# A hybrid encoder block in split fp32: each gate and up strip gets its weights at a place of its own

## The chip, the cores and the metric

The kernel runs on one core of one Trainium2 chip. The metric is the device time of one execution in microseconds. A profiled execution gives, beside its own time, a trace of every instruction; the span is the time from the first to the last instruction in it.

## The reference

One encoder block over 256 rows of width 2048: an input projection into four mixers (linear attention, Fourier mixing, long convolution, short convolution), an output projection, a cross attention over 256 memory rows, and a gated feed-forward layer of width 5632, each with a residual sum, and a final norm. All is fp32. What the change touches is the feed-forward layer:

```python
D_MODEL, SEQ, D_FF = 2048, 256, 5632

def rms_norm(x, g):
    xf = x.astype(jnp.float32)
    y = xf * lax.rsqrt(jnp.mean(xf * xf, axis=-1, keepdims=True) + EPS)
    return (y * g.astype(jnp.float32)).astype(x.dtype)

def swiglu(h, w_gate_up, w_down):
    gate, up = jnp.split(h @ w_gate_up, 2, axis=-1)
    return (jax.nn.silu(gate) * up) @ w_down

# in reference(), for the one layer:
x = x + mix @ w_out[l]
x = x + cross_attention(rms_norm(x, norm_g[l, 1]), mem_n, w_xq[l], w_xkv[l], w_xo[l])
x = x + swiglu(rms_norm(x, norm_g[l, 2]), w_gate_up[l], w_down[l])
return rms_norm(x, final_norm_g)
```

## The kernel before, in words

**Split products.** To multiply fp32 numbers with the faster `float32r` matmul, each operand is split into a high part (the value rounded to `float32r`) and a low part (the rest), and three products are added: high by high, high by low, low by high. Activations lie in slots `act` of 512 columns: the high part in columns 0 to 255, the low part in 256 to 511.

**The weight stream.** All weight matrices are cut into blocks of 128 x 128, and laid out in memory in the order in which the kernel takes them (`NBLK` blocks in all, 16 to a slab). `Stream._half` works half a slab at a time, 8 blocks or 1024 columns. For every second half it starts the load of a slab into one of three `raw` buffers from SP's queue (line 83). Then it takes a buffer `wh` and a buffer `wl`, each one of three, and fills them: the high part with a cast on ScalarE (line 104), the low part with a subtraction on VectorE (line 105). A buffer has 1088 columns of 4 bytes, of which 1024 are used; `at` is the column at which the used part starts. It is 0 in the stages listed in `ROWS`, among them everything from the gate and up projection on, and 8 in the others. `Stream.take` hands out the next blocks, and keeps the halves up to two ahead of the one in use (three while a fourth buffer, `extra`, exists, which is before the feed-forward layer).

**Two ways to multiply.** In `gemm` the weights are stationary and the activations stream past them (lines 301 and 302: 512 and 256 columns; lines 298, 299 and 302 in the narrow form: three times 256). In `gemm_rows`, the activations are stationary and a strip of 512 weight columns, four blocks, streams past them. For each of the 16 pieces of depth 128 and each half of the 256 rows, `part_rows` issues three matmuls of 512 columns (lines 346, 347 and 348):

```python
self.nc.tensor.matmul(p[:, :], hi, wh, start=start, stop=False)
self.nc.tensor.matmul(p[:, :], hi, wl, start=False, stop=False)
self.nc.tensor.matmul(p[:, :], lo, wh, start=False, stop=stop)
```

**The feed-forward layer.** `gate_up` goes through 11 pairs of strips: gate columns j x 512 and up columns j x 512. The first pair is taken in one call of `gemm_rows`, gate and up by turns at every depth; all later strips have a call of their own, gate before up:

```python
for j in range(1, DFF // 512):
    gate(self.gemm_rows("w_gate_up", [j * 512], self.h3)[0])
    up(j, self.gemm_rows("w_gate_up", [DFF + j * 512], self.h3)[0])
```

A strip is 16 x 4 = 64 blocks, or 8 halves. `gate` applies the activation function on ScalarE (line 757), `up` multiplies on VectorE, transposes (line 764) and writes the result to memory with four transfers from POOL's queue (line 767); `fetch` reads it back and splits it for the down projection (lines 779, 204 and 196). `down` then multiplies with four strips of 512 columns over 44 pieces of depth, again with `part_rows`. The last 32 blocks of the stream lie in buffers of their own (`held`).

The same lines 346 to 348 also serve two short stages earlier on: the values of the cross attention (99 to 202 us) and those of the linear attention (302 to 328 us).

The order of work on each engine is that of the program; `Background` puts side work (norms, transposes, the read-back) between the matmuls by estimated times. Lines 857 and 1119 are two such pieces of side work: small transposes and a small product of the long convolution.

Of the kernel before, what the change touches and what calls it, by code (L numbers as in the profile page):

```python
# [27 lines left out]
FT = DFF // P  # L28
EPS = 1e-6
NBLK = 16 * (40 + 16 + 16 + 32 + 16 + 88) + 16 * FT  # L30
# [6 lines left out]
HELD = 32  # L37

ROWS = ((256, 512), (768, 832), (NBLK - 48 * FT, NBLK))

LATE = 12

# [20 lines left out]
class Stream:  # L63
# [13 lines left out]
    def _half(self):  # L77

        nc, n = self.nc, 8 * len(self.halves)
        if n % 16 == 0:  # L80
            self.raw = self.rawp.tile([P, 2048], F32, name="raw", tag="raw")
            for a, b in zip(CUTS[n], CUTS[n][1:]) if n in CUTS else [(0, 1024), (1024, 2048)] if self.after else [(0, 2048)]:
                (nc.scalar if (n, a) == (0, 0) else nc.sync).dma_start(self.raw[:, a:b], self.W[n // 16][:, a:b])
                if self.after:
                    self.after.pop(0)()
        o = (n % 16) * P
        r = self.raw[:, o:o + 1024]
        if n >= NBLK - HELD:
            parts = []
            for a in (0, 512):  # L90
                wh, wl = self.places.pop(0)
                nc.scalar.copy(wh, r[:, a:a + 512])
                nc.vector.tensor_tensor(out=wl, in0=r[:, a:a + 512], in1=wh.bitcast(F32), op=ALU.subtract)
                parts.append((wh, wl))
            self.bg.dve(1024)
            self.halves.append(parts)
            return
        pool = self.extra if self.extra and len(self.halves) % 4 == 3 else self.wp
        wh, wl = (pool.tile([P, 1088], F32R, name=t, tag=t) for t in ("wh", "wl"))
        at = 0 if any(a <= n < b for a, b in ROWS) else 8  # L100
        wh, wl = wh[:, at:at + 1024], wl[:, at:at + 1024]
        edges = [0, 256, 512, 1024] if n == 0 else [0, 512, 1024] if n == 8 else [0, 1024]
        for a, b in zip(edges, edges[1:]):
            nc.scalar.copy(wh[:, a:b], r[:, a:b])  # L104
            nc.vector.tensor_tensor(out=wl[:, a:b], in0=r[:, a:b], in1=wh[:, a:b].bitcast(F32), op=ALU.subtract)  # L105
        self.bg.dve(1024)
        self.halves.append((wh, wl))
# [1326 lines left out]
```

## Time and profile before

| What | Value |
|---|---|
| Median of 2 runs | 1498.29 us (1498.02 to 1498.56) |
| Profiled execution, its own time | 1498.32 us |
| Its span | 1496.5 us |
| Granted TensorE clock, mean | 0.998 of full |
| TensorE busy | 1485.9 us (99%) |
| Weight loads | 1254.2 us (84%) |
| VectorE busy | 938.3 us (63%) |
| ScalarE busy | 759.3 us (51%) |
| GpSimd busy | 149.7 us (10%) |
| Moved by DMA | 306.11 MB, mean 205 GB/s |

A busy time counts every moment at which an instruction of the engine is under way. The matmuls of TensorE overlap one another, so their durations add up to more than the span that they fill; the distance between the starts of two matmuls tells the pace. The gate and up projection fills 761 to 1248 us, the down projection the rest up to 1488 us.

### The profile page before, as it was taken

What the parts mean: (1) busy time and instruction counts of PE and PEld (TensorE: products, weight loads), DVE (VectorE), ACT (ScalarE), POOL (GpSimd) and SP (SyncE); (2) the same over time, 40 slices, a digit from 0 to 9 for tenths busy, and PEclk for the clock granted to TensorE, in tenths of its full rate; (3) what the DMA queues carried; (4) which work ended last, traced back from release to release, by engine and by line L of the source; (5) the groups of instructions that cost most, each with busy time, mean ns of one, the idle gap of its engine ahead of it and who ended that gap; (6) DMA issues with size and microseconds to landing.
All of it is one profiled execution on the core that took longest, in us unless ns stands there. A gap on an engine that the chain in (4) does not pass through costs nothing.

```text
span 1496.5 us, 19811 instructions
## 1 busy us (share of the span) xinstructions
PE 1485.9 (99%) x7582; PEld 1254.2 (84%) x7582; DVE 938.3 (63%) x1373; ACT 759.3 (51%) x1125; POOL 149.7 (10%) x260
## 2 busy tenths in 40 slices
PE   9999999999999999999999999999999999999997
PEld 8887788889899888888888888888888888888886
DVE  6676778778777767877765554555554456444444
ACT  6565555557545655756544444444444445434344
POOL 0100100000000001200042401111110112000000
PEclk9999999999999999999999999999999999999999
DMA  9975554454546555554567756666666666555554
GB/s 355 347 250 193 189 192 160 167 192 142 183 142 222 188 185 201 193 179 152 189 194 253 239 207 213 216 223 225 209 204 211 220 222 226 185 186 194 197 196 141
DMA packets 56174, 306.11 MB, mean 205 GB/s; under 512 B 9197, under 2 KB 10510, under 8 KB 24464
## 3 DMA queue, kind: packets, MB, share of 16 engines
q1 hardware_dynamic: 45632, 281.11, 54.2%
q0 software_dynamic: 10016, 23.08, 4.9%
q8 instruction: 59, 0.97, 0.3%
q10 hardware_dynamic: 432, 0.66, 0.1%
q14 instruction: 35, 0.29, 0.1%
HBM read 291.18 MB, written 13.63 MB: 204 GB/s over the span
## 4 chain that ended last, share of the span: by engine, by line
PE 97%; ACT 1%; DVE 1%; DMA 0%; issue 0%; SPq 0%; ACTq 0%
PE pg L301 21%; PE pg L346 18%; PE pg L347 17%; PE pg L348 17%; PE pg L302 11%; PE pm L346 1%; PE pm L348 1%; PE pm L347 1%; PE pg L298 1%; PE pg L299 1%; PE pm L301 1%; PE pm L725 1%; PE pm L698 0%; PE pm L302 0%; DMA raw<-in_W 0%
## 5 line engine op out<-in xcount | busy, mean ns | idle before, releaser
L105 DVE TENSOR_TENSOR wl<-raw,wh 128x1024 fp32r<-128x1024 f32 (+1 forms) x503 | 611.6, 1217 | 481.5 <-ACT wh L104 477.1
L104 ACT CAST wh<-raw 128x1024 fp32r<-128x1024 f32 (+1 forms) x503 | 524.3, 1043 | 595.2 <-PE pg L348 396.3
L301 PE MATMUL pg<-act,wh 128*128 128x512 f32 x1296 | 457.7, 395 | 0.3 <-ACT wh L104 0.3
L302 PE MATMUL pg<-act,wl 128*128 128x256 f32 x1472 | 412.4, 280 | 0.2 <-DVE wl L105 0.2
L346 PE MATMUL pg<-wh,act 128*128 128x512 f32 x1008 | 397.1, 394 | 0.0
L347 PE MATMUL pg<-wl,act 128*128 128x512 f32 x1008 | 395.9, 393 | 0.0
L348 PE MATMUL pg<-wh,act 128*128 128x512 f32 x1008 | 392.9, 390 | 0.0
L301 PEld LDWEIGHTS pg<-act,wh 128*128 128x128 f32 x1296 | 243.6, 188 | 54.3 <-ACT wh L104 0.6
L302 PEld LDWEIGHTS pg<-act,wl 128*128 128x128 f32 x1472 | 276.8, 188 | 2.3 <-issue 1.2
L346 PEld LDWEIGHTS pg<-wh,act 128*128 128x128 f32 x1008 | 189.3, 188 | 45.8 <-issue 1.7
L348 PEld LDWEIGHTS pg<-wh,act 128*128 128x128 f32 x1008 | 189.3, 188 | 42.5
L347 PEld LDWEIGHTS pg<-wl,act 128*128 128x128 f32 x1008 | 189.5, 188 | 38.6
L767 POOL DMA_DIRECT2D hidden<-u x88 | 56.9, 654 | 312.1 <-DVE u L764 310.6
L298 PE MATMUL pg<-act,wh 128*128 128x256 f32 x176 | 50.6, 288 | 0.0
L299 PE MATMUL pg<-act,wh 128*128 128x256 f32 x176 | 49.3, 280 | 0.0
L346 PE MATMUL pg<-wh,f 128*128 128x512 f32 x120 | 47.3, 394 | 0.0
L348 PE MATMUL pg<-wh,f 128*128 128x512 f32 x120 | 47.0, 392 | 0.0
L347 PE MATMUL pg<-wl,f 128*128 128x512 f32 x120 | 46.6, 388 | 0.0
L811 POOL DMA_DIRECT2D xrows<-tmp x48 | 27.7, 584 | 130.1 <-DVE tmp L808 126.0
L196 DVE TENSOR_TENSOR tmp<-pg,tmp 128x256 f32<-128x256 f32 x86 | 35.9, 418 | 6.7 <-ACT tmp L308 4.5
L308 ACT COPY tmp<-pg 128x256 f32<-128x256 f32 x85 | 30.9, 365 | 10.9 <-PE pg L302 10.8
L298 PEld LDWEIGHTS pg<-act,wh 128*128 128x128 f32 x176 | 33.2, 188 | 0.2
(272 smaller groups left out, 1239.6 us busy)
## 6 DMA issues: line engine op xcount, KB each, us to landing
raw<-in_W SPq DMA_DIRECT2D x246, 1024.0 KB, 4.9
raw<-in_W SPq DMA_DIRECT2D x11, 512.0 KB, 7.5
hidden<-u POOLq DMA_DIRECT2D x88, 64.0 KB, 3.0
tmp<-hidden POOLq DMA_DIRECT2D x44, 128.0 KB, 4.0
res<-in_xT SPq DMA_DIRECT2D x8, 512.0 KB, 6.0
k<-in_mem SPq DMA_DIRECT2D x8, 256.0 KB, 7.8
k<-in_x SPq DMA_DIRECT2D x8, 256.0 KB, 8.4
keys<-tmp POOLq DMA_DIRECT2D x16, 128.0 KB, 5.8
```

The costliest lines, as they stand in the source:

```text
L104: nc.scalar.copy(wh[:, a:b], r[:, a:b])
L105: nc.vector.tensor_tensor(out=wl[:, a:b], in0=r[:, a:b], in1=wh[:, a:b].bitcast(F32), op=ALU.subtract)
L196: self.nc.vector.tensor_tensor(out=out, in0=a, in1=b, op=op)
L298: self.nc.tensor.matmul(p[:, 0:R], wh, slot[:, 0:R], start=start, stop=False)
L299: self.nc.tensor.matmul(p[:, 0:R], wh, slot[:, R:512], start=False, stop=False)
L301: self.nc.tensor.matmul(p[:, :], wh, slot[:, :], start=start, stop=False)
L302: self.nc.tensor.matmul(p[:, 0:R], wl, slot[:, 0:R], start=False, stop=stop)
L308: self.nc.scalar.copy(t, p[:, R:512])
L346: self.nc.tensor.matmul(p[:, :], hi, wh, start=start, stop=False)
L347: self.nc.tensor.matmul(p[:, :], hi, wl, start=False, stop=False)
L348: self.nc.tensor.matmul(p[:, :], lo, wh, start=False, stop=stop)
L767: nc.gpsimd.dma_start(to[:, :, 32 * a:32 * a + 32], u[32 * a:32 * a + 32, :].rearrange("f (b t) -> f b t", t=32))
```

## The change

A table of 22 places, one for each strip of 512 gate or up columns in the order in which the stream takes them, replaces the single `at` of these strips. The unit is a column of 4 bytes. Everything else, the buffers and their sizes included, stays.

```diff
 ROWS = ((256, 512), (768, 832), (NBLK - 48 * FT, NBLK))
+
+PLACES = (0, 0, 24, 32, 40, 48, 56, 8, 16, 4, 12, 20, 28, 36, 44, 52, 60, 2, 6, 22, 26, 24)
...
         pool = self.extra if self.extra and len(self.halves) % 4 == 3 else self.wp
         wh, wl = (pool.tile([P, 1088], F32R, name=t, tag=t) for t in ("wh", "wl"))
         at = 0 if any(a <= n < b for a, b in ROWS) else 8
+        if 0 <= n - (NBLK - 48 * FT) < 32 * FT:
+            at = PLACES[(n - (NBLK - 48 * FT)) // 64]
         wh, wl = wh[:, at:at + 1024], wl[:, at:at + 1024]
```

`NBLK - 48 * FT` is the first block of the gate and up projection, `32 * FT` the number of its blocks (`FT` is 44), and `n` the first block of a half.

## The prediction

> **What bounds the kernel now.** I read the page from the top: the share of each engine, the granted clock, the chain that ended last.
>
> ```profile
> span 1496.5 us, 19811 instructions
> PE 1485.9 (99%) x7582; PEld 1254.2 (84%) x7582; DVE 938.3 (63%) x1373; ACT 759.3 (51%) x1125; POOL 149.7 (10%) x260
> PEclk9999999999999999999999999999999999999999
> PE 97%; ACT 1%; DVE 1%; DMA 0%; issue 0%; SPq 0%; ACTq 0%
> PE pg L301 21%; PE pg L346 18%; PE pg L347 17%; PE pg L348 17%; PE pg L302 11%; PE pm L346 1%; PE pm L348 1%; PE pm L347 1%; PE pg L298 1%; PE pg L299 1%; PE pm L301 1%; PE pm L725 1%; PE pm L698 0%; PE pm L302 0%; DMA raw<-in_W 0%
> ```
>
> TensorE is busy all the way at an even clock, and the chain of waits is TensorE for 97%. Lines 346 to 348, in which a 512-column strip of split weights streams past a stationary piece of the activations, hold over half of it (18, 17 and 17%, and 3% more into the other PSUM pool). So the end is set by the distance from one matmul's start to the next one's. Next I asked for the groups of instructions in the stretch 807.9 to 1225.4 us, nineteen of the strips that the change touches:
>
> ```profile
> L347 PE MATMUL pg<-wl,act 128*128 128x512 f32 x608 | 239.6, 394 | 0.0
> L346 PE MATMUL pg<-wh,act 128*128 128x512 f32 x609 | 238.7, 392 | 0.0
> L348 PE MATMUL pg<-wh,act 128*128 128x512 f32 x609 | 236.3, 388 | 0.0
> L105 DVE TENSOR_TENSOR wl<-raw,wh 128x1024 fp32r<-128x1024 f32 x152 | 185.8, 1223 | 196.3 <-ACT wh L104 196.3
> L104 ACT CAST wh<-raw 128x1024 fp32r<-128x1024 f32 x152 | 159.1, 1047 | 227.8 <-PE pg L348 227.8
> L347 PEld LDWEIGHTS pg<-wl,act 128*128 128x128 f32 x609 | 114.5, 188 | 22.7
> ```
>
> TensorE waits for nothing there (0.0 idle), while the cast on ScalarE waits for TensorE to free a buffer and the subtraction on VectorE waits for the cast. The means (394, 392, 388 ns) are from issue to end and overlap; what counts is the step between starts. That is in the timeline, first of a gate strip, then of the value projection of the linear attention at 302.7 us. Columns are start, duration, instruction:
>
> ```profile
> 873.82 0.39 PE L346 MATMUL pg<-wh,act 128*128 128x512 f32 x1
> 874.05 0.39 PE L347 MATMUL pg<-wl,act 128*128 128x512 f32 x1
> 874.28 0.39 PE L348 MATMUL pg<-wh,act 128*128 128x512 f32 x1
> 874.51 0.39 PE L346 MATMUL pg<-wh,act 128*128 128x512 f32 x1
> ...
> 875.88 0.39 PE L346 MATMUL pg<-wh,act 128*128 128x512 f32 x1
> ```
>
> ```profile
> 302.67 0.40 PE L346 MATMUL pg<-wh,act 128*128 128x512 f32 x1
> 302.90 0.40 PE L347 MATMUL pg<-wl,act 128*128 128x512 f32 x1
> 303.14 0.40 PE L348 MATMUL pg<-wh,act 128*128 128x512 f32 x1
> 303.37 0.40 PE L346 MATMUL pg<-wh,act 128*128 128x512 f32 x1
> ...
> 304.77 0.40 PE L346 MATMUL pg<-wh,act 128*128 128x512 f32 x1
> ```
>
> Nine matmuls (three triples of lines 346, 347, 348) take 2.06 us in the gate strip and 2.10 us in the other place. By the start times in nanoseconds a triple is 686.7 ns in almost every strip from 807.9 to 1487 us, and 700.0 ns for 25 triples running from 302.67 us. The instructions, shapes, clock and buffers are the same. At 320.9 us sixteen small matmuls (line 1119) come between, and from then on the triples are mostly back at 687. So **the same matmul has at least two steady paces**, 228.9 and 233.3 ns, and keeps the one that it fell into until the train is broken. Neither VectorE nor ScalarE can be the reason, since the pace is constant to a nanosecond whether they run or not.
>
> **The change, part by part.** It adds and removes no instruction, no transfer and no wait. It moves the start of `wh` and `wl` within their buffers by 0 to 60 elements, for the 22 strips of the gate and up projection. Every instruction that touches them is priced in turn.
>
> *Which strips.* A half buffer is 8 blocks, a strip 64, so no half is shared between two strips. Strips 0 and 1 are interleaved in one call, and both have place 0: unchanged. The other 20 strips get places that are not 0. Each strip is 16 x 2 = 32 triples, so 20 x 32 = 640 triples or 1920 matmuls change; at 686.7 ns they are 439.5 us of the span.
>
> *The two writers.* A strip has 8 casts of 1047 ns and 8 subtractions of 1223 ns. Should the new places make them slower, the cover is this: a half lasts 12 matmuls x 228.9 = 2.75 us; the cast of a half starts when the half three before it is freed, so TensorE still has two halves, 5.49 us, while cast and subtraction need 1.05 + 1.22 = 2.27 us. Each could double before TensorE noticed (4.54 us). With that cover gone each such half would cost the excess; I take 0. The loads of `raw` on SP's queue, the transposes and the transfers on POOL's queue keep their place and their number: 0.
>
> *The stationary operand* is a slice of `act` and doesn't move; a weight load takes 188 ns beside a 229 ns matmul. Its relation to the moving operand does change, and that is part of the next term.
>
> *The moving operand.* This is the term that decides, and the trace of before has no matmul of this form at another place: a buffer is 1088 x 4 = 4352 = 17 x 256 bytes and a half of a strip 2048 bytes, so before the change all starts in these strips have one remainder modulo 256 bytes. I bound it by the nearest rows. *Below*: the steps of a triple are not equal; in most strips they are some 229, 232 and 226 ns in turn, and 226 is the shortest that this form shows. With 226 for all three a triple is 678 ns: 640 x (-8.7) = -5.6 us. A floor under that: in the stages with stationary weights the step falls from 230 ns at 512 columns (line 301) to 118 at 256 (line 302), 0.4375 ns for a column, so 512 columns alone take 224 of the 228.9 ns, and no more than 640 x 3 x 4.9 = 9.4 us can be had. *Above*: the other pace seen for the same instruction, 700 ns: 640 x 13.3 = +8.5 us. Wider still, the triples of lines 298, 299 and 302 (three times 256 columns) are spread from 350 to 361 ns, 3.1%: 3.1% of 439.5 = +13.6 us.
>
> Which one? The pace of 700 appears where a train of these matmuls starts straight behind matmuls with other operand places and no gap (99.1 us and 302.7 us). In the changed kernel a strip begins behind one with another place, with no gap. That is the nearest row, so I take 700 for a strip whose place is new in kind and 687 for the rest. New in kind: every 512-column operand that streams in the split matmuls starts, in the kernel as laid out, at a multiple of 64 bytes. Of the 20 places only 16, 32 and 48 elements keep that. So 17 strips x 32 = 544 triples x 13.3 ns = **+7.2 us**, and 3 strips at 0. The end of the last strip is broken by the transposes of line 857 (1246.0 us), so the down projection should keep 687; if not, it adds 352 x 13.3 = 4.7 us.
>
> Sum: the profiled execution took 1498.32 us (span 1496.5 and 1.8 around it), and the median of the runs shown is 1498.29. With +7.2 this is **1505.5 us**.
>
> [...] The trace doesn't bear out a single pace, as the 687 and 700 above show; no run here shows yet what a place does.
>
> **The rivals.** *A: place doesn't matter*, and the two paces come only from how a train begins. For it: all strips but the disturbed ones take 21.97 us, whichever of three buffers they use. Against it: one remainder for all of them is just what would hide the effect. Time: 1498.3; not slower than before. *B: a better pace.* The new distances between the streamed and the stationary start take the longer steps of a triple down to the shortest, 226, in all 20 strips: 1498.3 - 5.6 = 1492.7. For it: two of three steps do have something to lose; place 24 (used twice) gives, modulo 256, the distance between streamed and stationary start that the stages with stationary weights have. Against: 18 other strips have other distances. It decides if more strips get faster than slower. *C: a real clash.* At some places the weight load and the stream collide, and the 128 columns of the load delay the stream by as much: 128 x 0.4375 = 56 ns per matmul. With a quarter of the places (5 strips, 480 matmuls) it is +27 us, 1525; with all of them +107 us. Over 2% from 6 strips on. For it: a load takes 188 of 229 ns, so the two always run together. Against: no steady train of split matmuls shows such a step; the longer ones of lines 1033 and 1034 (about 320 and 427 ns) alternate full and half stationary pieces, which isn't done here. *D: the change doesn't reach the instructions.* The index follows the order in which the strips are taken, and 60 + 1024 fits in 1088; I give it no weight.
>
> **How the numbers follow.** Forecast (some strips slower by one or a few such steps, 1501 to 1514) 0.55; A 0.19; B 0.13; C 0.13, of which half passes 2%. A measurement of this kernel can tell about 2% from no change, 30 us: 1468 to 1528. Slower by over 2%: 0.07, from C. Faster by over 2% would need 47 ns off each triple, where the floor above leaves 3 x 4.9 = 15: 0.01. Within 2%: 0.92. The range takes in B's end, 1492.7, and the lower part of C: 1492.5 to 1524.
>
> **What would show it.** Right: same instruction counts; strips from 807.9 us on whose length differs from place to place, near 21.97 us for 16, 32 and 48 and near 22.4 us for others; TensorE still at 0.0 idle on lines 346 to 348; casts and subtractions near 1047 and 1223 ns. Wrong: all strips at 21.97 (A), most below it (B), single strips over 25 us (C), or an idle time of TensorE that ends with the subtraction of line 105, which would mean that the writers and not the reads had slowed.

## The result and the profile after

The changed kernel takes 1505.59 us (median of 2 runs, 1504.83 to 1506.34), against 1498.29 before: ratio 1.0051, 95% interval 1.0031 to 1.0071. The forecast was 1505.5. The profiled execution took 1504.83 us, 6.5 more than the one before.

The page and the chain of waits say what they said before: TensorE is busy (99%) at an even clock (0.999 on average), and it is the chain (97%). Only the span has grown, from 1496.5 to 1503.0 us. Four lines were added above, so 346 to 348 are now 350 to 352, and 104 and 105 are 108 and 109.

```profile
span 1503.0 us, 19811 instructions
PE 1492.7 (99%) x7582; PEld 1254.4 (83%) x7582; DVE 938.7 (62%) x1373; ACT 760.8 (51%) x1125; POOL 150.1 (10%) x260
PEclk9999999999999999999999999999999999999999
PE 97%; ACT 1%; DVE 1%; DMA 0%; issue 0%; SPq 0%; ACTq 0%; DVEq 0%
```

The groups of instructions from 805.3 to 1230 us, which are nineteen of the strips with new places:

```profile
L350 PE MATMUL pg<-wh,act 128*128 128x512 f32 x608 | 240.5, 396 | 0.0
L352 PE MATMUL pg<-wh,act 128*128 128x512 f32 x608 | 240.2, 395 | 0.0
L351 PE MATMUL pg<-wl,act 128*128 128x512 f32 x608 | 239.7, 394 | 0.0
L109 DVE TENSOR_TENSOR wl<-raw,wh 128x1024 fp32r<-128x1024 f32 x152 | 185.9, 1223 | 203.3 <-ACT wh L108 203.3
L108 ACT CAST wh<-raw 128x1024 fp32r<-128x1024 f32 x152 | 159.5, 1049 | 234.6 <-PE pg L352 234.6
```

TensorE still waits for nothing (0.0), and the cast and the subtraction take as long as before (1049 and 1223 ns; 1047 and 1223 before). The matmuls themselves are longer: 396, 394 and 395 ns for the three lines in their order, against 392, 394 and 388. The timeline shows it strip by strip; these are the first matmuls of three strips and of the strips behind two of them:

```profile
850.26 0.40 PE L350 MATMUL pg<-wh,act 128*128 128x512 f32 x1
...
872.65 0.39 PE L350 MATMUL pg<-wh,act 128*128 128x512 f32 x1
...
894.44 0.40 PE L350 MATMUL pg<-wh,act 128*128 128x512 f32 x1
...
1073.10 0.40 PE L350 MATMUL pg<-wh,act 128*128 128x512 f32 x1
...
1095.79 0.39 PE L350 MATMUL pg<-wh,act 128*128 128x512 f32 x1
```

By these lines, rounded to 0.01 us, the strip at place 40 takes 22.39 us, the next one, at 48, 21.79, and the one at 44 takes 22.69. Before, every undisturbed strip took 21.97. The lengths of all 20 strips, from the same differences, taken in nanoseconds, are below. The first one has the break by the transposes (line 861, 857 before) at its start, with which it took 22.10 us before; the last one is given without the transposes at its end, with which it takes 22.84 (22.34 before).

| Place | 24 | 32 | 40 | 48 | 56 | 8 | 16 | 4 | 12 | 20 |
|---|---|---|---|---|---|---|---|---|---|---|
| us | 22.59 | 22.41 | 22.40 | 21.78 | 22.40 | 22.39 | 22.40 | 22.19 | 22.19 | 22.39 |

| Place | 28 | 36 | 44 | 52 | 60 | 2 | 6 | 22 | 26 | 24 |
|---|---|---|---|---|---|---|---|---|---|---|
| us | 22.18 | 22.52 | 22.69 | 22.23 | 22.08 | 22.61 | 22.35 | 22.44 | 22.52 | 22.49 |

With the transposes at the end they add up to 447.59 us, against 439.96 for the same 20 strips before: +7.63. The stages ahead of the feed-forward layer, which the change does not touch, took 1.1 us less in this execution, and the rest is equal: +6.5 in the span. So the place of the streamed operand, the only thing that was changed, alters the pace of matmuls that wait for nothing. One place is faster than before (21.78 us against 21.97), nineteen strips are slower (22.08 to 22.69).

### The profile page after: what moved, and what is told of

It reads as the page before. It is cut to its first block, busy times and chain, and to the rows that moved or that the text cites. A ratio compares the mean times of both kernels' runs of the same rounds, so it can differ in the third digit from the quotient of the medians.

```text
span 1503.0 us, 19811 instructions
## 1 busy us (share of the span) xinstructions
PE 1492.7 (99%) x7582; PEld 1254.4 (83%) x7582; DVE 938.7 (62%) x1373; ACT 760.8 (51%) x1125; POOL 150.1 (10%) x260
## 4 chain that ended last, share of the span: by engine, by line
PE 97%; ACT 1%; DVE 1%; DMA 0%; issue 0%; SPq 0%; ACTq 0%; DVEq 0%
PE pg L305 20%; PE pg L350 17%; PE pg L352 17%; PE pg L351 17%; PE pg L306 11%; PE pm L352 1%; PE pm L351 1%; PE pm L350 1%; PE pg L302 1%; PE pg L303 1%; PE pm L305 1%; PE pm L729 1%; PE pm L702 0%; PE pm L306 0%; DMA raw<-in_W 0%
```

## The experiments

Two questions were open. What of a place counts: the streamed start by itself, its distance from the stationary start, or just what stood before in the train? And can the one good place be used? In the tables of places the order is that of the strips, and a strip of 32 triples at 680.0, 686.7, 700.0 and 710.0 ns a triple takes 21.76, 21.97, 22.40 and 22.72 us.

**Good places behind bad ones.**

```diff
-PLACES = (0, 0, 24, 32, 40, 48, 56, 8, 16, 4, 12, 20, 28, 36, 44, 52, 60, 2, 6, 22, 26, 24)
+PLACES = (0, 0, 24, 0, 44, 0, 16, 0, 48, 0, 8, 0, 2, 0, 32, 48, 44, 48, 24, 48, 60, 0)
```

> The same strips with the table 0, 0, 24, 0, 44, 0, 16, 0, 48, 0, 8, 0, 2, 0, 32, 48, 44, 48, 24, 48, 60, 0: place 0 or 48 behind each of several others, with no break in the train. Theory P, a strip's length is set by its own place: every later strip at 0 takes 21.97 us and every one at 48 takes 21.78, whatever went before; 24 takes about 22.5, 44 22.7, 16 and 32 and 8 22.4, 2 22.6, 60 22.1. Theory H, the pace is inherited from the strip before (as the 700 ns triples from 302.67 us suggest): a strip at 0 behind 24, 44, 16, 8 or 2 keeps 22.4 us or more, and lengths follow the order and not the place.

The timeline, from the first matmul of the strip at 48 to the strip at 0 behind it and the one behind that:

```profile
939.38 0.40 PE L350 MATMUL pg<-wh,act 128*128 128x512 f32 x1
...
961.19 0.40 PE L350 MATMUL pg<-wh,act 128*128 128x512 f32 x1
...
983.18 0.39 PE L350 MATMUL pg<-wh,act 128*128 128x512 f32 x1
```

48 takes 21.81 us and 0 takes 21.99. The six later strips at 0 with no break took 21.98 to 21.99, behind 24, 44, 16, 48, 8 and 2 alike; the seventh, behind 60, has the transposes at its end and took 22.34, as the last strip did in the kernel before. The four at 48 took 21.76 to 21.81. So in these strips the two places do not inherit: theory P holds for them here. Elsewhere it doesn't quite. Place 44 took 22.69 us behind 0 but 22.40 behind 48, and place 60, 22.08 in the changed kernel, took 22.40 behind 48.

**The stationary operand moved instead.** The table is that of the changed kernel; all activation slots lie 64 bytes, or 16 places, higher. The small tiles behind them, among them the residuals and constants, move by as much, up to the second gap, which shrinks by 64 bytes so that the weight buffers stay; none of these tiles is an operand of the strips' matmuls.

```diff
+        self.gap(cp, 64)
         self.act = [cp.tile([P, 512], F32R, name=f"act{i}") for i in range(24)]
...
-        self.gap(cp, 224)
+        self.gap(cp, 160)
```

> The changed kernel with its table as it is, but all stationary activations moved up by 64 bytes (16 elements) in SBUF. Theory R, the distance between the streamed start and the stationary start counts, modulo 256 bytes: each strip behaves like the place 16 lower in the run of the changed kernel, so the strips at 0 take about 21.8 us (as 48 did), 16 takes 21.97, 48 takes 22.4, 12 takes 22.1, 60 takes 22.7, 36 and 24 22.4. Theory M, the start of the streamed operand alone counts: every strip keeps its length (0 21.97, 48 21.78, 44 22.7). A third case: neither pattern, if both starts count each by itself. Stages before the feed-forward layer, where the activations stream, may change as well; the strips are read by themselves.

The first matmuls of the strips at 16 and at 60 and of those behind them:

```profile
945.83 0.39 PE L350 MATMUL pg<-wh,act 128*128 128x512 f32 x1
...
967.80 0.39 PE L350 MATMUL pg<-wh,act 128*128 128x512 f32 x1
...
1123.59 0.40 PE L350 MATMUL pg<-wh,act 128*128 128x512 f32 x1
...
1146.27 0.40 PE L350 MATMUL pg<-wh,act 128*128 128x512 f32 x1
```

Place 16 now takes 21.97 us, as 0 did, and 60 takes 22.68, as 44 did. The rest follows: 52 took 22.52 (36 before the shift: 22.52), 4 took 22.24 (52: 22.23), 12 took 22.08 (60: 22.08), 20 took 22.18 (4: 22.19). Strip 1, at 0, took 21.77 up to the transposes, about what 48 took (21.78). Of the 17 strips from the third on whose counterpart is in the table above, 15 agree with it to 0.02 us. The two others are the strip right behind the transposes, 22.51 with that break against 22.39, and the one at 32, 22.31, which is what 16 took in the run before this (22.32; 22.40 in the table). The streamed start did not move in this run, so theory M falls: **in these strips, what counts of a place is the distance of the streamed start from the stationary start, modulo 256 bytes.** The 256 bytes are 64 places: 16 places below 4 and 12 would be -12 and -4, and what 4 and 12 took (22.24 and 22.08 us) is what 52 and 60 had taken (22.23 and 22.08), 64 places above those. With half of that 16 and 48 would be alike, which took 22.40 and 21.78 before the shift. As laid out, the two are equal modulo 256 bytes at place 48, and 64 bytes apart at place 0.

The run took 1509.02 us as a whole (one run). Its feed-forward layer begins 6.4 us later than in the changed kernel. In the stages ahead of it the activations mostly stream past stationary weights, and a pair of lines 305 and 306 took 352.3 ns on average instead of 346.8, which over some 1330 such pairs is 7.3 us; the triples of the value stages, at 680 ns now, give some of it back. So the pace of the stages with stationary weights changed with the start of an operand, too.

**High and low part at different places.**

```diff
-PLACES = (0, 0, 24, 32, ...)
+PLACES = ((0, 0), (0, 0), (48, 0), (0, 48), (16, 0), (0, 16), ..., (48, 44), (44, 48))
...
-        wh, wl = wh[:, at:at + 1024], wl[:, at:at + 1024]
+        wh, wl = (x[:, a:a + 1024] for x, a in zip((wh, wl), at))
```

> High and low parts get places of their own: pairs (48,0), (0,48), (16,0), (0,16), (32,0), (0,32), (8,0), (0,8), (24,0), (0,24), (44,0), (0,44), (2,0), (0,2), (60,0), (0,60), (12,0), (0,12), (48,44), (44,48) for the strips after the first two. If each matmul pays for its own streamed start, the high part (two of three matmuls) carries two thirds of what a place cost in the changed kernel and the low part one third: (16,0) +0.28 us over 21.97 and (0,16) +0.14; (44,0) +0.47 and (0,44) +0.24; (48,0) -0.13 and (0,48) -0.06. If the pace is a rhythm of the whole triple, the two parts don't add up to the whole.

The first matmuls of the strip at (0,48) and of the one behind it:

```profile
828.47 0.40 PE L350 MATMUL pg<-wh,act 128*128 128x512 f32 x1
...
850.87 0.40 PE L350 MATMUL pg<-wh,act 128*128 128x512 f32 x1
```

The parts do not add up. With the high part at 48 and the low part at 0 a strip took 22.37 us (with the break by the transposes in it), the other way round 22.40. Yet 48 for both takes 21.78, and 0 for both 21.97. (16,0) took 22.30 and (0,16) 22.29, some three quarters of the loss each (16 for both: 22.40), not two thirds and one third. (44,48), the last strip, took 22.18 without the transposes at its end, and (48,44) 22.55. So a matmul did not pay for its own start alone here, by which (48,0) and (0,48) were expected at 21.84 and 21.91 us; the pace belonged to the triple as a sequence. What stood before a strip was not varied here.

**All strips at the good place.**

```diff
+PLACES = (48,) * 22
```

> All 22 strips at place 48, the only one that was faster in the changed kernel. Theory P: every undisturbed strip takes 21.78 us, 0.19 less than before; 22 x 0.19 = 4.2 us less than before, about 1494.1 us. Theory H: without changes of place the train falls back to 21.97 after the first break, and the time is that of before, 1498.3.

1493.70 us, ratio 0.9971 (0.9960 to 0.9982) to the kernel before. Every undisturbed strip took 21.76 us, all 32 triples of most strips exactly 680 ns. Theory P gave 1494.1. The first matmuls of two strips:

```profile
870.40 0.39 PE L350 MATMUL pg<-wh,act 128*128 128x512 f32 x1
...
892.16 0.39 PE L350 MATMUL pg<-wh,act 128*128 128x512 f32 x1
```

**All streaming stages at the good place.** From the kernel before; the buffers of the last 32 blocks move with them.

```diff
-        at = 0 if any(a <= n < b for a, b in ROWS) else 8
+        at = 48 if any(a <= n < b for a, b in ROWS) else 8
...
-                self.gap(hp, 64)
```

> From the kernel before: place 48 in all stages that stream split weights (gate, up, down, the values of both attentions), and the buffers of the last 32 blocks moved to the same remainder. Streamed and stationary starts are then equal modulo 256 bytes in every such triple. Theory R with the floor at equal starts: every triple takes 680.0 ns, 6.67 less than before; gate and up -4.3 us, down 352 x 6.67 = -2.3, the value stages 160 triples, some of them at 700 before, -1.1 to -1.5: about 1490.3 us. If 48 helped gate and up alone: about 1494.

1490.45 us, ratio 0.9951 (0.9938 to 0.9963). The down projection has the new pace too; from its timeline, nine matmuls apart:

```profile
1270.00 0.39 PE L346 MATMUL pg<-wh,f 128*128 128x512 f32 x1
...
1272.04 0.39 PE L346 MATMUL pg<-wh,f 128*128 128x512 f32 x1
```

2.04 us, three triples of 680, where the gate strip before took 2.06. This version beats both kernels. It is 7.4 us below the 1497.89 that the kernel before took beside it, where counting triples gave 7.7 to 8.1.

**The good place in the other stages as well.**

```diff
-        at = 48 if any(a <= n < b for a, b in ROWS) else 8
+        at = 48
```

> As the run with place 48 in all streaming stages, but place 48 in the stages with stationary weights too (8 before). If equal starts are best for any split matmul, a pair of lines 301 and 302 stays at 346.7 ns or gets shorter, and the time is 1490 or less. If the best distance belongs to the rhythm of a stage (a triple of 512 columns, a pair of 512 and 256), the pairs get longer than 346.7 and the time rises by some us over the other run.

1492.79 us, ratio 0.9964 (0.9950 to 0.9977). The intervals of the two runs overlap, but the pairs of lines 301 and 302 tell more: 349.4 ns on average against 346.8, with nearly all single pairs between 343 and 361. So equal starts are not best for every sequence: the triple of 512 columns took 680.0 ns at distance 0, the least seen, while the pair of 512 and 256 took less at the distance that it had (346.8 ns) than at the two others tried, in this run (349.4) and with the shifted activations (352.3).

**All strips at the slowest place of the table.**

```diff
+PLACES = (44,) * 22
```

> All 22 strips at place 44, the slowest of the changed kernel. Theory P alone: every strip 22.69 us, 22 x 0.71 = 15.7 us over before, 1513.9. If this place has two rhythms and the one of 700.0 ns (seen for it behind place 48) holds: 22.40 us a strip, +9.4, 1507.7. Theory H: back to 1498.3.

Ten executions fell into two groups of five: 1494.49 to 1496.22 us and 1513.64 to 1514.26. The slower group lies where theory P put it (1513.9); the faster one lies below all three forecasts. The median, 1504.93, and the ratio, 1.0049 (1.0011 to 1.0088), describe neither. The profiled execution (1495.24 us) shows how. First matmuls of strip 1 and strip 4, the transposes that end strip 1, and the strip behind strip 4:

```profile
784.42 0.40 PE L350 MATMUL pg<-wh,act 128*128 128x512 f32 x1
...
807.14 0.38 PE L861 MATMUL pm<-ident,res 128*128 128x128 f32 x2
...
851.25 0.39 PE L350 MATMUL pg<-wh,act 128*128 128x512 f32 x1
...
873.01 0.39 PE L350 MATMUL pg<-wh,act 128*128 128x512 f32 x1
```

Up to the transposes a strip takes 22.72 us; behind them it takes 21.76, at the same place, for all of the 20 strips left but for the breaks in the first and the last. Were those 20 to stay at 710 ns, they would take 19.2 us more; the medians of the groups are 18.7 apart. No profile was taken of an execution of the slower group, so that it stays at 710 is inferred from its time.

**Rhythms that are kept.**

```diff
+PLACES = (0, 0, 48, 44, 44, 44, 44, 0, 44, 44, 44, 44, 48, 60, 60, 60, 0, 60, 60, 60, 16, 16)
```

> Runs of four strips at place 44 behind one strip at 48 and behind one at 0, and runs of three strips at place 60 behind 48 and behind 0; the table is 0, 0, 48, 44 x4, 0, 44 x4, 48, 60 x3, 0, 60 x3, 16 x2. Theory K, a place has a few rhythms, the train enters one of them by what went before and keeps it until it is broken: all four strips at 44 behind 48 take 22.40 us and all four behind 0 take 22.69; the strips at 60 take 22.40 behind 48 and 22.08 behind 0, to the last one. Theory P, the place alone with a short settling: the second to the fourth strip of a run take the same length whatever stands ahead of the run.

Second strip at 44 behind 48, and second strip at 44 behind 0, each with the strip that follows:

```profile
850.25 0.40 PE L350 MATMUL pg<-wh,act 128*128 128x512 f32 x1
...
872.65 0.40 PE L350 MATMUL pg<-wh,act 128*128 128x512 f32 x1
...
962.13 0.40 PE L350 MATMUL pg<-wh,act 128*128 128x512 f32 x1
...
984.85 0.40 PE L350 MATMUL pg<-wh,act 128*128 128x512 f32 x1
```

22.40 against 22.72 us. All four strips behind 48 took 22.40; behind 0 the first took 22.70 and the other three 22.72. Place 60 took 22.40 three times behind 48 and 22.08 three times behind 0. So theory K holds in this run, and theory P's short settling does not: with the run before, place 44 has three rhythms (680, 700 and 710 ns), place 60 has two, and a train kept the one that it entered for the three or four strips at that place.

**Places between.**

```diff
+PLACES = (0, 0, 46, 50, 47, 49, 45, 54, 58, 62, 1, 10, 14, 18, 30, 34, 38, 42, 0, 60, 48, 60)
```

> Places that no strip had so far, mostly near the best one: 46, 50, 47, 49, 45, 54, 58, 62, 1, 10, 14, 18, 30, 34, 38, 42, then 0, 60, 48, 60. From the run with shifted activations, theory R gives in advance: 50 as its place 2, 22.51 us; 54 as its 6, 22.40; 10 as its 26, 22.08. If only equal starts are good, 46, 47, 49 and 50 are far above 21.76 already; if it is a smooth valley, they lie between 21.76 and 21.97. Place 60 behind 0 and behind 48 shows whether one place has two rhythms (22.08 and 22.40 so far).

54 took 22.40 and 10 took 22.08, as foretold from the shifted run; 50 took 22.36 and not 22.51. There is no smooth valley around 48: 47 took 21.88, while 46 (with the break by the transposes), 45 and 49 took 22.35, 22.95 and 22.82. Place 60 took 22.08 behind 0 and, without the transposes at its end, 22.40 behind 48.

**A break ahead of each strip.** All strips at 44.

```diff
         nk = len(slots)
+        if w == "w_gate_up":
+            self.nc.tensor.matmul(self.bank()[:, 0:1], self.ones, self.ones[:, 0:1], start=True, stop=True)
```

> All strips at place 44, and a matmul of one column on other operands ahead of each strip, which breaks the train 21 times. Theory K: the rhythm is chosen anew at each break, so strips of 21.8, 22.4 and 22.7 us (680, 700, 710 ns a triple) may all occur within one execution, each holding to its end, plus 0.1 to 0.3 us for each break; the executions, which with place 44 and no breaks came out at either 1495 or 1514 us, now lie closer together. If instead the choice is made once for an execution, all strips of one have the same length and the two groups of times stay 19 us apart.

This tells less than was meant. By the trace, sixteen of the added matmuls (two instructions each) ran in one heap from 807.1 to 810.7 us:

```profile
807.12 3.63 PE L361 MATMUL pm<-ones 128*128 128x1 f32 x32
```

The transposes that end strip 1 in the other runs came only behind the last strip here, at 1267.5 us. Behind the heap the granted clock was 0.51 from 810.6 to 813.7 us and the matmuls lay 427 ns apart; then strip 2 went on at 710 ns a triple, and so did all strips after it. Apart from strip 2 only the last four were broken at their start. Behind each of these four breaks the 710 ns came back (22.79 to 22.80 us with the break). The times were 1514.56 to 1521.49 us. So none of these five breaks chose another rhythm, where theory K had expected a choice at each, while the transposes were followed by another one in the profiled execution with all strips at 44 and no added matmul. This trace also shows that a train at place 44 can hold 710 ns to the end of the strips, as was inferred for the slower group there. What makes the choice at a break is open.

## Why the prediction was right, and where it was not

**The bound** was read rightly: nothing but the step between matmul starts moved, with 0.0 idle on TensorE and writers as fast as before. That the two writers, the queues and the transfers cost nothing held.

**The term of the moving operand** came out at the right size: +7.2 us foretold, +7.63 in the 20 strips, of which 1.1 was covered in the profiled execution by earlier stages that the change does not touch; +7.3 between the medians. The other pace, 700 ns, was the right row to take: six of the 20 strips lie at 22.39 to 22.41 us, and the mean of all 20 is 22.36.

**The step that failed is the choice of strips.** It said that starts off a multiple of 64 bytes are new in kind and slow, and that 16, 32 and 48 keep 687. Measured, 16 and 32 took 22.40 and 22.41, and 48 took 21.78. The shifted run shows why the criterion was wrong: with the streamed start where it was, place 16 took 21.97 us instead of 22.40 once the stationary start had moved by 64 bytes, so the distance of the two counts and not the streamed start's own alignment. So the sum held partly by luck. The 17 strips were foretold at +0.43 each and had +0.41 on average, but for another reason than the one given, and singly from +0.11 to +0.71; the three others, foretold at 0, had +0.43, +0.43 and -0.19. These errors cancelled but for 0.4 us.

**That a pace is inherited** was half right. It is for 44 (22.40 us behind 48, 22.69 to 22.72 behind 0) and for 60 (22.40 and 22.08). In the strips, places 0 and 48 returned to their own pace behind every place tried (21.98 to 21.99 and 21.76 to 21.81 us). But the value projection at 302.7 us, which stayed at 700 ns until broken, also lies at place 0 and so at the same distance: behind the stage with stationary weights even this place had a second pace.

**The rivals.** A (place doesn't matter) fell. Moving the stationary operand by 64 bytes moved the lengths of the strips along the table by the same 16 places as moving the stream; the same matmul took 226.7 ns (a third of 680.0) to 239.1 ns (22.95 us over the 96 matmuls of the strip at place 45) by the distance of the two and by what stood before. Whether the reads of the streamed and of the stationary operand meet anywhere, or whether the weight load takes anything from the stream at all, no run here shows. B (a better pace) is what place 48 does, and its price was near: 678 ns assumed, 680.0 measured. As a forecast for this table it was wrong, since one strip of 20 has it. C (a clash that stretches a strip past 25 us) did not occur; the longest unbroken strip was 22.95, at place 45.

## What to carry to other kernels

When matmuls run back to back and wait for nothing, as these did (0.0 us idle), look at the start addresses of their operands. Here a strip took from 21.76 us (place 48) to 22.95 (place 45) by the distance of the streamed and the stationary start modulo 256 bytes and by what stood before. Put the two starts at a distance chosen by a table of places in one run: a single strip at place 48 told 680.0 from 686.7 ns a triple in the trace, a difference of 0.19 us, while eleven executions of the kernel before lay between 1497.14 and 1498.55. The distance belongs to the sequence of matmuls (0 for the triple here, at 680.0 ns; the best of three tried for the pair was another, at 346.8 ns against 349.4 and 352.3), and with the high part alone, or the low part alone, at the good place the gain was lost here (22.37 and 22.40 us against 21.78). Time a chosen place in several executions: place 44 looked good in some (1494.49 us) and bad in others (1514.26), since it has several rhythms.

## What was not expected of the hardware

In these runs, trains of matmuls that wait for nothing (0.0 us idle) settled to constant paces and kept them: 680.0, 686.7, 700.0 or 710.0 ns a triple on average in the strips that settled best, held from four strips in a row (700.0) to twenty (680.0 and 710.0). Other places had other paces in the changed kernel, such as 690.0 at 60 and 693.3 at 4, 12 and 28, and at some the triples of one strip differed among themselves, by turns 700, 703, 702 and 706 ns or so at 24, and 700 and 693 at 6. And one program, all strips at 44, at a granted clock of 0.998 to 0.999 had two times, 1495 and 1514 us, most likely because its train entered one rhythm or the other behind the same transposes; only several executions, or the trace, show that this is neither noise nor the clock.
